# One decoder layer on Trainium2: split operands that stand still placed 64 bytes into their tiles, and the last two input blocks of the channel stage made earlier

## The chip, the cores and the metric

The kernel runs on one core of a Trainium2 chip. TensorE (PE) multiplies: an operand that stands still (stationary, at most 128 rows by 128 columns) is loaded into it, and another (moving, up to 512 columns) streams past. VectorE (DVE), ScalarE (ACT) and GpSimd (POOL) work on tiles in the on-chip memory, and DMA queues move data between it and the device's memory. The metric is the time of one execution on the device, in microseconds (us).

## The reference

```python
def reference(x, c, ...):                       # x (1, 2048, 1024) f32, D_FF = 2816
    mod = silu(c) @ w_ada + b_ada
    sh1, sc1, g1, sh2, sc2, g2 = split(mod, 6)
    u = rmsnorm(x, norm1_w) * (1 + sc1) + sh1
    hq, hf, hi, hg, aq, ak, av = split(u @ w_in)
    mix = concat([hgrn2(...), diff_attention(...)]) @ w_out
    h = x + g1 * mix
    u = rmsnorm(h, norm2_w) * (1 + sc2) + sh2
    ff = (silu(u @ w_ffn_gate) * (u @ w_ffn_up)) @ w_ffn_down
    return rmsnorm(h + g2 * ff, final_norm_w)
```

The mixer has a linear recurrence with four heads (hgrn2) and a differential attention with four heads. Everything is in 32-bit floats.

## The kernel before

**Split operands.** A 32-bit operand is cast to fp32r (the "high" part, ACT, L125), and DVE subtracts that from the operand for the "low" part (L126). A product is three matmuls: high by high, low by high, high by low. Both parts come from `split_tile`, whose tiles are 128 columns longer than their content. So where the content begins in its tile can be chosen, and the argument `moving` does that: content that moves begins SHIFT = 16 floats, which is 64 bytes, into the tile, and other content at the tile's start. As the program is laid out, every such tile itself begins at a multiple of 128 bytes. Only the weights that `load_half` makes for `proj_tf` (L195) are given moving=True: there 256 columns of weights move past, 64 bytes off, and 128 columns of an input stand still at a multiple of 128 bytes. In all other matmuls of split operands both begin at a multiple of 128 bytes. In the rows the moving operand is named first, then the one that stands still (ps_hg<-cuh,wh).

**The first half of the program** (up to 1401 us in the profile) computes projections, recurrence, attention and the output projection, on four blocks of 512 tokens, from block 3 to block 0. `proj_ft` (L183) is a projection with the weights standing still and 512 columns of the input moving, `proj_tf` (L195) one in pieces of 256 moving columns. `project_out(b)` writes block b of h to the device's memory, and `make_u2(b)` reads it back, norms it, transposes it on PE (128 x 128, L228), scales it (ACT L560, DVE L556) and writes u2 there as eight tiles (`u2_d`, L561).

**The second half** is the channel sub-layer, in two stages: s = 1 takes blocks 3 and 2, s = 0 blocks 1 and 0. Each stage has `combine(s)`, `activations(s)` and `down(s)`. The matrix products are done as two-by-two block products with seven multiplications instead of eight. `combine` makes the sums and differences of the u2 blocks that the seven products take: x, t2, t3, y, t1, w and t4, as split tiles named cx, ct2, ct3, cy, ct4, and cu for both t1 and w. `activations` goes over p = 0 to 10. For each p, `seven` runs on the gate's weights and then on those of the up projection. `seven` loads two strips of weights on SP's queue (r1, r2), builds sums s1 to s4 from them (buffers `wsum`), splits them (wa, ws, wt and the small wb), and runs seven products of 12 matmuls, 512 wide (L997), with the weights standing still and the combined inputs moving. The sums of products stand in PSUM banks: x and y in acc, t3 and t4 in sc, t1 and w in hg, t2 in tr or pv by turns. ws goes to t2 and t1, wt to t3 and w, wb to t4. `weights(p)`, in stage 1, also prepares the down projection's combined weights. `down(s)` takes the activations as the operand that stands still and the weights as the moving one (L1202), 77 steps of 24 matmuls, adds the residual, and does the final norm: squares with their sum on ACT (L1142), then scale and store.

**What sets the order.** Each engine takes its instructions in order. The program is written as generators that are interleaved by hand, and a list scheduler orders the instructions of each engine by estimated times before the program is built. In the second half the written order is: `combine(1)`, with most of it inside `project_out(0)`; `activations(1)`; `make_u2(1)`, `make_u2(0)`; `down(1)`, with `most` of `combine(0)` woven in; then `rest` of `combine(0)` beside the norms of stage 1; `activations(0)`; `down(0)`. As scheduled, the transposes of `make_u2(1)` and `make_u2(0)` stand among the first 160 matmuls of `down(1)`. SP's queue loads weights in order; POOL's queue stores.

Of the kernel before, what the change touches and what calls it, by code (L numbers as in the profile page):

```python
# [38 lines left out]
LAST = 2  # L39
LAST0 = 4  # L40
# [8 lines left out]
def kernel(ctx: ExitStack, tc: tile.TileContext, io: dict, out: bass.AP):  # L49
# [63 lines left out]
    u2_d = [[dram.tile([P, TB], F32, name=f"u2d{b}_{k}") for k in range(NK)] for b in range(NTB)]  # L113
# [110 lines left out]
    def transposed(k, xts, tags):  # L224
        pt = bank(*alternate("tr", *tags))
# [276 lines left out]
    def project_out(b, px, o, g1, take=None, tmp_=None):  # L502
# [11 lines left out]
        for k in range(NK):  # L514
            pt = transposed(k, ots, (("hg", 2),))
# [33 lines left out]
    def make_u2(b, px, take=None, tmp_=None):  # L549

        xts = normed(px, [h_d[b][tt * P:(tt + 1) * P] for tt in range(NT)], take)
        for k in range(NK):
            pt = transposed(k, xts, (("tr", 1), ("pv", 1)))
            ut = tmp_() if tmp_ else px.tile([P, TB], F32, name="t512", tag="t512", bufs=2)
# [6 lines left out]
            POOL.dma_start(out=u2_d[b][k], in_=ut)  # L561
# [309 lines left out]
    def combine(s):  # L871
# [15 lines left out]
        def load(kk, half, late, queue=SP):  # L887
            t = temp()
            queue.dma_start(out=t, in_=u2_d[2 * s + late][kk + 4 * half])
# [21 lines left out]
        def rest():  # L911
            for kk in range(4):
# [3 lines left out]
                put("w", kk, load(kk, 1, 1))  # L916
# [26 lines left out]
        return made, together(), most(), rest()  # L943
# [9 lines left out]
    def split_big(raw):  # L953
        wh, wl = (split_tile(pf, t, t, NW) for t in ("wh2", "wl2"))
# [12 lines left out]
    def seven(src, fs, u, finish):  # L967


# [4 lines left out]
        a11, a12 = r1[:, :TB], r1[:, TB:]  # L974
        a21, a22 = r2[:, :TB], r2[:, TB:]
        wa = split_big(r1)
        sa, sb = big("wsum", "wsum", 2), big("wsum", "wsum", 2)
        s1, s2, s3, s4 = sa[:, :TB], sa[:, TB:], sb[:, :TB], sb[:, TB:]
        DVE.tensor_tensor(s1, a21, a22, op=ALU.add)
        DVE.tensor_tensor(s2, s1, a11, op=ALU.subtract)  # L980
        ws = split_big(sa)
        DVE.tensor_tensor(s3, a11, a21, op=ALU.subtract)
        DVE.tensor_tensor(s4, a12, s2, op=ALU.subtract)
        wt = split_big(sb)
        wb = split_small(a22)
# [27 lines left out]
        finish(0, 0, px_, None)  # L1013
        product(pv_, half(ws, 0), "t1", True)
# [3 lines left out]
        t12 = temp()  # L1018
        DVE.tensor_tensor(t12, pv_, c12, op=ALU.add)
        finish(0, 1, None, t12)  # L1020
        product(pz, wb, "t4", False)
        DVE.tensor_tensor(c12, pz, c12, op=ALU.add)
        finish(1, 0, None, c12)
# [13 lines left out]
    def activations(s, u):  # L1037

        for p in range(NP):
# [11 lines left out]
            def other():  # L1051
                return ss.tile([P, TB], F32, name="asum", tag="asum", bufs=4)

            def up(j, t, ps, sb):
                a = sl[j, t]
                DVE.tensor_tensor(a, sb if ps is None else ps, a, op=ALU.mult)
                if (j, t) == (0, 0):
                    store(0, a)
                elif (j, t) == (1, 1):
                    store(5, a)  # L1060
                elif (j, t) == (0, 1):
                    s1, s2 = other(), other()
                    DVE.tensor_tensor(s1, a, sl[1, 1], op=ALU.add)
                    store(4, s1)
                    DVE.tensor_tensor(s2, s1, sl[0, 0], op=ALU.subtract)
                    store(1, s2)
# [218 lines left out]
```

## Time and profile before

| what | us |
| --- | --- |
| median of 3 runs | 2706.44 (2706.34 to 2708.68) |
| profiled execution | 2710.17 |
| its span in the profile | 2708.4 |
| PE busy in the span | 2605.8 (96%) |
| ACT, DVE busy in the span | 1144.6, 1826.3 |

The profiled execution took 1.8 us more than its span, and 3.7 us more than the median. The share of PE is so high that the time is PE's: its instructions one behind the other, and the few places where it stands. The second half of the span, by stage: `project_out(0)`, `make_u2(2)` and the start of `combine(1)` end at 1401 us; `activations(1)` runs to about 1829; `down(1)` to 2052; `activations(0)` to about 2484; `down(0)` to 2693.9; then 14.5 us without matmuls.

### The profile page before, as it was taken

To read this page: it belongs to the slowest core of one execution; us is meant where nothing else is said; L and a number is where in the kernel's file an instruction comes from. 1 tells how busy PE (TensorE), PEld (TensorE's weight loads), DVE (VectorE), ACT (ScalarE), POOL (GpSimd) and SP (SyncE) were. 2 spreads that over 40 slices of the span, in tenths; PEclk is the share of its full clock that TensorE was granted. 3 is DMA by queue.
4 is the path that set the end of the run, shared out by engine and by line. 5 is a ranking of instruction groups with operands and counts; after the bars stand their busy time and mean duration, and the time that the engine had idled before them with its cause. 6 is when DMAs were issued, how large, how long until landed. Compare 5 with 4: busy or idle time off the path is not lost.

```text
span 2708.4 us, 40567 instructions
## 1 busy us (share of the span) xinstructions
PE 2605.8 (96%) x14753; PEld 2267.6 (84%) x14753; DVE 1826.3 (67%) x3608; ACT 1144.6 (42%) x2050; POOL 385.6 (14%) x603
## 2 busy tenths in 40 slices
PE   6999989999999999898899999999998999999997
PEld 5888879999999998798888888887887888888886
DVE  7434457778778778865577777667778666665467
ACT  4542126665565565643343222235444222222434
POOL 2552200010100001012121111112002110001001
PEclk9999999999999999998999999999999999999999
DMA  8764672433334231456665444459656333235665
GB/s 281 262 218 167 220 241 83 148 99 111 108 110 154 77 98 47 137 184 221 200 217 167 167 167 156 139 192 342 221 185 220 113 106 98 101 109 205 199 187 179
DMA packets 333628, 449.17 MB, mean 166 GB/s; under 512 B 26810, under 2 KB 212460, under 8 KB 333300
## 3 DMA queue, kind: packets, MB, share of 16 engines
q1 hardware_dynamic: 295508, 324.39, 37.6%
q0 software_dynamic: 37920, 122.19, 11.9%
q8 instruction: 116, 1.90, 0.3%
q14 instruction: 84, 0.69, 0.1%
HBM read 326.41 MB, written 120.06 MB: 165 GB/s over the span
## 4 chain that ended last, share of the span: by engine, by line
PE 72%; DMA 4%; issue 4%; DVE 3%; ACT 1%; POOL 1%; SPq 1%; DVEq 0%; POOLq 0%; ACTq 0%
PE ps_hg L997 8%; PE ps_sc L997 8%; PE ps_acc L997 8%; PE ps_acc L195 8%; PE ps_acc L183 6%; PE ps_pv L654 4%; PE ps_sc L1202 4%; PE ps_acc L1202 4%; PE ps_hg L1202 3%; PE ps_tr L997 2%; PE ps_sc L624 2%; PE ps_tr L650 2%; PE ps_sc L625 2%; PE ps_pv L997 2%; PE ps_hg L716 2%
## 5 line engine op out<-in xcount | busy, mean ns | idle before, releaser
L125 ACT CAST wh<-wraw 128x1024 fp32r<-128x1024 f32 (+1 forms) x320 | 327.1, 1044 | 589.3 <-PE ps_hg L997 183.2
L126 DVE TENSOR_TENSOR wl<-wraw,wh 128x1024 fp32r<-128x1024 f32 (+1 forms) x320 | 383.7, 1213 | 187.9 <-ACT wh L125 186.0
L195 PE MATMUL ps_acc<-wh,uh 128*128 128x256 f32 x1040 | 294.6, 285 | 1.0 <-ACT uh L526 0.8
L195 PE MATMUL ps_acc<-wl,uh 128*128 128x256 f32 x1040 | 292.8, 283 | 2.6 <-DVE wl L126 2.6
L195 PE MATMUL ps_acc<-wh,ul 128*128 128x256 f32 x1040 | 291.5, 283 | 0.1
L125 ACT CAST wh<-wsum 128x1024 fp32r<-128x1024 f32 x88 | 92.6, 1053 | 310.5 <-PE ps_acc L997 129.7
L195 PEld LDWEIGHTS ps_acc<-wl,uh 128*128 128x128 f32 x1040 | 196.0, 189 | 5.3 <-DVE wl L126 2.8
L195 PEld LDWEIGHTS ps_acc<-wh,uh 128*128 128x128 f32 x1040 | 195.8, 189 | 4.0 <-ACT uh L526 1.6
L195 PEld LDWEIGHTS ps_acc<-wh,ul 128*128 128x128 f32 x1040 | 195.1, 189 | 2.6 <-DVE ul L527 0.3
L628 DVE CUSTOM_DVE_ANT_0 s<-ps_sc,dist,mx 128x512 f32<-128x512 f32 x192 | 143.5, 747 | 46.8 <-PE ps_sc L625 42.4
L633 ACT ACTIVATE s<-s,mx 128x2048 f32<-128x2048 f32 (+15 forms) x128 | 154.1, 1204 | 47.2 <-DVE mx L628 45.2
L654 PE MATMUL ps_pv<-vt,wt 128*128 128x128 f32 x1088 | 152.0, 280 | 2.8 <-ACT wt L652 2.2
L654 PEld LDWEIGHTS ps_pv<-vt,wt 128*128 128x128 f32 x1088 | 141.6, 195 | 10.3 <-ACT wt L652 4.9
L183 PE MATMUL ps_acc<-uh,wh 128*128 128x512 f32 x352 | 140.3, 400 | 1.3 <-ACT wh L125 1.3
L183 PE MATMUL ps_acc<-ul,wh 128*128 128x512 f32 x352 | 139.8, 398 | 0.6 <-DMA ul<-ud 0.6
L183 PE MATMUL ps_acc<-uh,wl 128*128 128x512 f32 x352 | 138.5, 395 | 1.1 <-DVE wl L126 1.1
L997 PE MATMUL ps_hg<-cuh,wh 128*128 128x512 f32 x352 | 137.2, 391 | 1.1 <-ACT cuh L125 0.8
L624 PE MATMUL ps_sc<-ks,q 128*128 128x512 f32 (+2 forms) x320 | 133.3, 419 | 4.4 <-DVE mx L628 3.6
L997 PE MATMUL ps_hg<-cul,wh 128*128 128x512 f32 x352 | 137.4, 390 | 0.1
L997 PE MATMUL ps_hg<-cuh,wl 128*128 128x512 f32 x352 | 137.1, 390 | 0.0
L652 ACT COPY wt<-ps_tr 128x512 f32<-128x512 f32 (+3 forms) x160 | 83.1, 520 | 108.1 <-PE ps_tr L650 106.8
L126 DVE TENSOR_TENSOR wl<-wsum,wh 128x1024 fp32r<-128x1024 f32 x88 | 107.3, 1221 | 29.9 <-ACT wh L125 29.1
(424 smaller groups left out, 6811.4 us busy)
## 6 DMA issues: line engine op xcount, KB each, us to landing
wraw<-in_w_in_dram SPq DMA_DIRECT2D x88, 512.0 KB, 4.0
wraw<-actd SPq DMA_DIRECT2D x154, 256.0 KB, 2.6
wraw<-in_w_ffn_gate_dram SPq DMA_DIRECT2D x44, 512.0 KB, 4.9
wraw<-in_w_ffn_up_dram SPq DMA_DIRECT2D x44, 512.0 KB, 3.6
actd<-t POOLq DMA_DIRECT2D x88, 256.0 KB, 3.1
wraw<-wdd SPq DMA_DIRECT2D x88, 256.0 KB, 4.0
actd<-asum POOLq DMA_DIRECT2D x66, 256.0 KB, 3.5
wraw<-in_w_ffn_down_dram SPq DMA_DIRECT2D x66, 256.0 KB, 4.0
```

Source lines behind the costliest of these rows:

```text
L125: ACT.copy(dst_h, src)
L126: DVE.tensor_tensor(dst_l, src, dst_h.bitcast(F32), op=ALU.subtract)
L183: PE.matmul(pa, a[:, k % 4, j * P:(j + 1) * P], c, start=n == 0, stop=n == 3 * NK - 1)
L195: PE.matmul(pa[:, j], a[:, tt * P:(tt + 1) * P], c[:, k % 4], start=n == 0, stop=n == 3 * NK - 1)
L624: PE.matmul(ps[:, :n], qs[m][0][:, qc], ks[m][pc][:, :n], start=True, stop=False)
L625: PE.matmul(ps[:, :n], qs[m][1][:, qc], ks[m][pc][:, :n], start=False, stop=True)
L628: DVE.tensor_tensor_reduce(out=s[:, lo:hi], in0=ps[:, :hi - lo], in1=dist[:, u0_:u0_ + hi - lo], op0=ALU.add, op1=ALU.min, scale=-slope, s ...
L633: ACT.activation(s[:, :W], s[:, :W], AF.Exp, scale=-1.0, bias=mx[:, npiece - 1:npiece], accum_out=mx[:, 4:5])
L652: ACT.copy(wt[:, :ge - g], pt[:, :ge - g])
L654: PE.matmul(pv[:, :P], wt[:, j - g], vq[j // 4][:, j % 4], start=j == 0, stop=j == i)
L997: PE.matmul(pa[:, cs], a, c[:, cs], start=first and i == 0, stop=i == 11 and cs.stop == TB, skip_group_check=not first)
L1202: PE.matmul(sets[n % 2][tt], a[x][:, tt * P:(tt + 1) * P], w[y], start=kk == 0 and m == 0 and n not in (2, 6), stop=kk == NP - 1 and m == ...
```

## The change

1. **Where split operands begin.** The argument is now `shift`, true unless told otherwise. Shifted by 64 bytes: all wide tiles of `load_half` (so also the weights that stand still in `proj_ft`, 960 matmuls), and the tiles of `split_big`, which are the weights that stand still in `seven` and the activations that stand still in `down`. The moving weights of `down` are not (`not w`), nor is the small wb of `seven` (product t4), nor are the moving inputs. `proj_tf` is as it was.
2. **u2 of blocks 1 and 0.** `make_u2(1)` and `make_u2(0)` before `down(1)` are gone. A new generator `u2_tile` makes one token tile (128 rows) of one block in each p = 2 to 9 of `activations(1)`: its norm ahead of the gate's `seven`, four transposes and four ACT scalings between gate and up, four more after up. `u2_d` has another layout, and is written in rows of 512 bytes.
3. **Weights ahead.** What `seven` did first (load, s1, s2, split of wa and ws) is `prepare`. For p = 0 it runs before the stage: in stage 1 before the last steps of `combine(1)`, in stage 0 inside `down(1)`.
4. **Rest of combine(0).** It falls into `last_w`, now inside `down(1)`, and `last_t1`, which runs with the norms of stage 1 in a callback after the first `seven` of `activations(0)` has split its weights.
5. **Order of the products in `seven`:** x, t2, t3, y, t1, w, t4 becomes x, t2, t3, y, t4, t1, w, with one more temporary (c21). In `up` the sums of the activations follow that order.
6. **Banks.** The transposes of `project_out(0)` alternate over hg, hg, sc, sc and not over hg alone.
7. LAST 2 to 1, LAST0 4 to 3, and another order of slots in `down`. Of PE's order at the end of both `down` stages these change nothing.

```diff
-LAST = 2
-LAST0 = 4
+LAST = 1
+LAST0 = 3
...
-    def split_tile(pool, name, tag, bufs, moving=False, wide=True):
-
-        n = moving * SHIFT
+    def split_tile(pool, name, tag, bufs, shift=True, wide=True):
+
+        n = (shift and wide) * SHIFT
         return pool.tile([P, D + wide * P], F32R, name=name, tag=tag, bufs=bufs)[:, n:n + D]
...
-            split_tile(pool, n, t, bufs, moving, wide).rearrange("p (k c) -> p k c", k=4)
+            split_tile(pool, n, t, bufs, True, wide).rearrange("p (k c) -> p k c", k=4)
...
-        def rest():
+        def last_w():
+            for kk in range(4):
+                put("w", kk, load(kk, 1, 1))
+                yield
+
+        def last_t1():
             for kk in range(4):
                 x, z = load(kk, 0, 0), load(kk, 0, 1)
                 DVE.tensor_tensor(x, z, x, op=ALU.subtract)
                 put("t1", kk, x)
-                put("w", kk, load(kk, 1, 1))
                 yield
...
-    def split_big(raw):
-        wh, wl = (split_tile(pf, t, t, NW) for t in ("wh2", "wl2"))
+    def split_big(raw, shift=True):
+        wh, wl = (split_tile(pf, t, t, NW, shift) for t in ("wh2", "wl2"))
...
+    def prepare(src, fs):
...
         wa = split_big(r1)
...
+        return r1, r2, wa, s2, split_big(sa)
...
+    def u2_tile(b, tt):
+        def take(dt=F32):
+            t = pf.tile([P, D], dt, name="xt1", tag="g1", bufs=1)
+            return t[:, :TB], t[:, TB:]
+
+        xt, = normed(ss, [h_d[b][tt * P:(tt + 1) * P]], take)
+        yield
+        for g, tag in enumerate(("tr", "pv")):
+            pt = bank(tag, 1, (4, P))
+            for k in range(4):
+                PE.transpose(out=pt[:, k], in_=xt[g][:, k * P:(k + 1) * P], identity=ident)
+            ut = other()
...
+            yield
...
             fs = (p, p + NP)
-            seven(w_gate, fs, u, gate)
+            q = p - 2
+            u2 = u2_tile(1 - q // 4, q % 4) if s and 0 <= q < 8 else iter(())
+            next(u2, None)
+            seven(first if p == 0 else prepare(w_gate, fs), u, gate, between if p == 0 else None)
             if s:
                 weights(p)
-            seven(w_up, fs, u, up)
+            next(u2, None)
+            seven(prepare(w_up, fs), u, up)
+            next(u2, None)
...
-                ops.append(split_big(raw))
+                ops.append(split_big(raw, not w))
...
+    weights0 = prepare(w_gate, (0, NP))
     run(steps)
-    activations(1, made)
-    make_u2(1, ss, slots(T3), temp)
-    make_u2(0, ss, slots(T2), temp)
-    made, _, most, rest = combine(0)
+    activations(1, made, weights0)
+    made, _, most, last_w, last_t1 = combine(0)
     steps = down_load(1, 0) + down_load(1, 2)
-    _, norms = down(1, steps, itertools.chain([None] * 8, most))
-    run(calls(*norms), rest)
-    activations(0, made)
+    weights0, norms = down(
+        1, steps, itertools.chain([None] * 8, most, [None] * 13, last_w), lambda: prepare(w_gate, (0, NP))
+    )
+    activations(0, made, weights0, lambda: run(calls(*norms), last_t1))
```

PE, end of `project_out(0)` (L195), where `make_u2(2)` (xt) and the transposes of the mixer's output (slot) stand between the matmuls. Before:

```order
L195 MATMUL ps_acc<-wh,slot 128x256 x2
L228 MATMUL ps_pv<-ident,xt 128x128 x4
L228 MATMUL ps_hg<-ident,slot 128x128 x4
L228 MATMUL ps_tr<-ident,xt 128x128 x4
L228 MATMUL ps_hg<-ident,slot 128x128 x4
L195 MATMUL ps_acc<-wh,slot 128x256
```

And in the changed kernel:

```order
L195 MATMUL ps_acc<-wh,slot 128x256 x2
L228 MATMUL ps_tr<-ident,xt 128x128 x4
L228 MATMUL ps_pv<-ident,xt 128x128 x4
L228 MATMUL ps_hg<-ident,slot 128x128 x8
L228 MATMUL ps_sc<-ident,slot 128x128 x8
L195 MATMUL ps_acc<-wh,slot 128x256
```

The 16 transposes of the mixer's output that stood in groups of four around matmuls stand together, on two kinds of bank, and 24 matmuls of L195 stand ahead of them where 12 did.

PE, start of `down(1)`; slot in L228 is the normed tile of `make_u2`, L997 the last products of `activations(1)`. Before:

```order
L1202 MATMUL ps_acc<-wl_19206,wh_19198 128x512
L1202 MATMUL ps_acc<-wh_19205,wl_19199 128x512
L228 MATMUL ps_tr<-ident,slot 128x128
L228 MATMUL ps_pv<-ident,slot 128x128
L1202 MATMUL ps_acc<-wl_19206,wh_19198 128x512
L997 MATMUL ps_hg<-cuh_15464,wh_18823 128x512
```

In the changed kernel the same place reads:

```order
L1235 MATMUL ps_acc<-wh_19221,wh_19214 128x512
L1235 MATMUL ps_acc<-wl_19222,wh_19214 128x512
L1235 MATMUL ps_acc<-wh_19221,wl_19215 128x512
L1006 MATMUL ps_hg<-cuh_15440,wh_19087 128x512
L1006 MATMUL ps_hg<-cul_15441,wh_19087 128x512
```

The 64 transposes of `make_u2(1)` and `make_u2(0)` are gone from here; as L1058, in eight pairs of groups of four, they stand between the products of `activations(1)`.

ACT, end of `down(1)` and start of `activations(0)`; the casts from wsum are those of the first ws and wt. Before:

```order
L125 CAST wh_21089<-wraw_21085 128x1024
L125 CAST wh_21097<-wsum 128x1024
L125 CAST sh<-wraw_21216 128x512
L1142 ACTIVATE junk,fss<-slot 128x512 x6
L125 CAST wh_21103<-wsum 128x1024
L125 CAST wh_21218<-wraw_21214 128x1024
L1142 ACTIVATE junk,fss<-slot 128x512
L125 CAST cuh_21036<-t_21034 128x512
```

In the changed kernel:

```order
L125 CAST wh_20993<-wraw_20989 128x1024
L125 CAST wh_21000<-wsum 128x1024
L125 CAST sh<-wraw_21232 128x512
L1175 ACTIVATE junk,fss<-slot 128x512 x4
L1015 COPY t_21144<-ps_acc 128x512
L1175 ACTIVATE junk,fss<-slot 128x512
L125 CAST wh_21031<-wsum 128x1024
L125 CAST wh_21234<-wraw_21230 128x1024
```

Ahead of the cast of wt there are now five of the norm's squares and the eviction of product x, where there were six squares. On PE the 12 matmuls of product y (cy) stand ahead of product t3, which takes wt; before they stood behind it.

## Rows read from the trace of the kernel before

**Rows 1.** The page: busy time of each engine and its share of the span.

```profile
PE 2605.8 (96%) x14753; PEld 2267.6 (84%) x14753; DVE 1826.3 (67%) x3608; ACT 1144.6 (42%) x2050; POOL 385.6 (14%) x603
```

**Rows 2.** Busy time by stretch: start:end, length, then the first line's columns.

```profile
core 0: us, PE busy (x) PEld busy (x) DVE busy (x) ACT busy (x) POOL busy (x), PEclk, DMA share, GB/s
1339.00:1362.00 23.00, 16.97 (x116) 15.64 (x115) 12.85 (x20) 10.05 (x18) 4.57 (x8) 0.85 0.47 161
1365.00:1400.00 35.00, 35.00 (x300) 35.00 (x299) 28.76 (x42) 11.10 (x15) 11.08 (x18) 1.00 0.69 236
1401.10:1432.00 30.90, 27.38 (x105) 19.57 (x104) 29.98 (x47) 18.07 (x29) 5.02 (x10) 0.94 0.60 188
1432.00:1823.00 391.00, 391.00 (x1744) 324.17 (x1743) 274.32 (x385) 110.77 (x148) 59.98 (x111) 1.00 0.49 164
1823.00:1892.00 69.00, 64.74 (x311) 52.18 (x309) 49.94 (x82) 42.60 (x72) 20.19 (x30) 1.00 0.95 351
2052.20:2095.00 42.80, 34.83 (x140) 26.84 (x140) 36.66 (x62) 19.32 (x35) 7.32 (x12) 0.92 0.58 190
2095.00:2480.00 385.00, 385.00 (x1718) 319.21 (x1717) 246.50 (x341) 107.08 (x141) 38.39 (x71) 1.00 0.31 105
```

**Rows 3.** Timeline of PE at the lower clock: start, us, engine, line, operation.

```profile
2065.99 0.63 PE L997 MATMUL ps_sc<-ct3l,wh 128*128 128x512 f32 x1
...
2067.26 0.63 PE L997 MATMUL ps_sc<-ct3l,wh 128*128 128x512 f32 x1
```

**Rows 4.** Timeline of PE at full clock, in down(0) and in activations(1).

```profile
2601.85 0.39 PE L1202 MATMUL ps_hg<-wh,wh 128*128 128x512 f32 x1
...
2603.89 0.39 PE L1202 MATMUL ps_acc<-wh,wh 128*128 128x512 f32 x1
...
1500.11 0.39 PE L997 MATMUL ps_sc<-ct4l,sh 128*128 128x512 f32 x1
...
1502.38 0.39 PE L997 MATMUL ps_sc<-ct4h,sl 128*128 128x512 f32 x1
```

**Rows 5.** Timeline of PE, L195: usual spacing, and the closest one.

```profile
1380.53 0.40 PE L195 MATMUL ps_acc<-wh,slot 128*128 128x256 f32 x2
...
1382.30 0.40 PE L195 MATMUL ps_acc<-wh,slot 128*128 128x256 f32 x2
...
452.43 0.28 PE L195 MATMUL ps_acc<-wh,uh 128*128 128x256 f32 x1
...
453.11 0.28 PE L195 MATMUL ps_acc<-wh,uh 128*128 128x256 f32 x1
```

**Rows 6.** Timeline of PE and DVE before the transposes of make_u2(2).

```profile
1352.77 0.44 PE L228 MATMUL ps_pv<-ident,xt 128*128 128x128 f32 x1 [4.05 <-DVE t L556]
...
1351.81 0.81 DVE L556 TENSOR_SCALAR t<-ps_pv,a,modc 128x512 f32<-128x512 f32 x1 [3.65 <-DMA u2d<-t]
```

**Rows 7.** What PE waited for, from 1395 us on: in total, times, longest.

```profile
PE ps_sc L997 <- ACT wh L125: 4.2, 1, 4.2
PE ps_acc L997 <- ACT t L1006: 2.8, 2, 1.8
PE ps_acc L1202 <- ACT wh L125: 1.5, 1, 1.5
PE ps_hg L1202 <- DVE wl L126: 1.5, 2, 1.2
...
PE ps_pv L1202 <- DVE t L556: 0.9, 1, 0.9
```

**Rows 8.** Timeline of ACT and of PE at the start of activations(0).

```profile
2056.58 0.63 ACT L1142 ACTIVATE junk<-slot 128x512 bf16<-128x512 f32 x1 [3.56 <-DVE slot L1135]
...
2060.98 1.03 ACT L125 CAST wh<-wsum 128x1024 fp32r<-128x1024 f32 x1
...
2057.49 0.39 PE L997 MATMUL ps_pv<-ct2h,wl 128*128 128x512 f32 x1
2062.06 0.79 PE L997 MATMUL ps_sc<-ct3h,wh 128*128 128x512 f32 x1 [4.18 <-ACT wh L125]
```

More of the change, by code (lines that the diff above doesn't have):

```diff
@@ L112 @@
     gate_d = [dram.tile([P, D], F32, name=f"gated{j}") for j in range(2)]
-    u2_d = [[dram.tile([P, TB], F32, name=f"u2d{b}_{k}") for k in range(NK)] for b in range(NTB)]
+    u2_d = [[dram.tile([P, 4, TB], F32, name=f"u2d{b}_{k}") for k in range(2)] for b in range(NTB)]
     act_d = [
@@ L224, in transposed @@
     def transposed(k, xts, tags):
-        pt = bank(*alternate("tr", *tags))
+        pt = bank(*alternate(tags, *tags))
         for tt in range(NT):
@@ L499, in run, with project_out @@
                 pass
-    def project_out(b, px, o, g1, take=None, tmp_=None):
+    def project_out(b, px, o, g1, take=None, tmp_=None, tags=(("hg", 2),)):
         def half():
@@ L547, in project_out, with make_u2 @@
             yield
-    def make_u2(b, px, take=None, tmp_=None):
-        xts = normed(px, [h_d[b][tt * P:(tt + 1) * P] for tt in range(NT)], take)
+    def make_u2(b, px, tags=(("tr", 1), ("pv", 1))):
+        xts = normed(px, [h_d[b][tt * P:(tt + 1) * P] for tt in range(NT)])
         for k in range(NK):
-            pt = transposed(k, xts, (("tr", 1), ("pv", 1)))
-            ut = tmp_() if tmp_ else px.tile([P, TB], F32, name="t512", tag="t512", bufs=2)
+            pt = transposed(k, xts, tags)
+            ut = px.tile([P, TB], F32, name="t512", tag="t512", bufs=2)
             if k % 2:
@@ L888, in load @@
             t = temp()
-            queue.dma_start(out=t, in_=u2_d[2 * s + late][kk + 4 * half])
+            queue.dma_start(out=t, in_=u2_d[2 * s + late][half][:, kk])
             return t
@@ L941, in together @@
                 yield
-        return made, together(), most(), rest()
+        return made, together(), most(), last_w(), last_t1()
     def big(name, tag, bufs, dt=F32):
@@ L1013, in seven @@
         finish(0, 0, px_, None)
+        product(pz, wb, "t4", False)
+        c21 = temp()
+        DVE.tensor_tensor(c21, pz, c12, op=ALU.add)
+        finish(1, 0, None, c21)
         product(pv_, half(ws, 0), "t1", True)
@@ L1017, in seven @@
         product(pv_, half(wt, 1), "w", False)
[L1018 to L1023, printed above, removed]
+        DVE.tensor_tensor(c12, pv_, c12, op=ALU.add)
+        finish(0, 1, None, c12)
     def weights(k):
@@ L1035, in weights, with other, activations @@
             POOL.dma_start(out=wd_d[n][k], in_=t)
-    def activations(s, u):
+    def u2_tile(b, tt):
[9 more added lines that the diff above has]
+            ut = other()
+            for k in range(4):
+                n = 4 * g + k
+                ACT.activation(
+                    ut[:, k * P:(k + 1) * P], pt[:, k], AF.Identity, bias=modc[:, SH2, n:n + 1], scale=a2[:, n:n + 1]
+                )
+            POOL.dma_start(
+                out=u2_d[b][g][:, :, tt * P:(tt + 1) * P], in_=ut.rearrange("p (k n) -> p k n", n=P)
+            )
+            yield
+    def other():
+        return ss.tile([P, TB], F32, name="asum", tag="asum", bufs=4)
+    def activations(s, u, first, between=None):
         for p in range(NP):
@@ L1116, in down @@
                 [bank("hg", 2), bank("hg", 2), bank("pv", 1), bank("tr", 1)]]
-        place = slots([f"u{z}{k}" for z in "hl" for k in range(NK)])
+        place = slots([f"u{z}{k}" for ks in (range(4, NK), range(4)) for z in "hl" for k in ks])
         ho = [[place() for tt in range(NT)] for t in range(2)]
@@ L1211, in down @@
             held = []
-            if n == 6 and k == 0 and not s:
+            if n == 6 and k == 0:
                 for tt in range(NT):
@@ L1216, in down @@
             pass
-        return made, [lambda t=t, tt=tt: norm(t, tt, POOL) for t in (1, 0) for tt in range(NT)] if s else []
+        return made, [lambda tt=tt: norm(0, tt, POOL) for tt in range(NT)] if s else []
     def calls(*fs):
```

64 lines of the change are left out of this document (29 added, 35 removed).

## The prediction, made before the changed kernel ran

> **What bounds the kernel now.** I began with busy time: PE is busy for 96% of the span, DVE for 67% and ACT for 42% [rows 1]. So two things can shorten the time: PE's matmuls coming closer together, and the few places where PE stands or runs at its lower clock. The table by stage shows where those places are [rows 2]. In 1432:1823 and in 2095:2480 PE is busy without a break at clock 1.00; there only the spacing of matmuls counts. It stands, or has a lower clock, in four short stretches: 1339:1362 (16.97 of 23.00 us busy, clock 0.85), 1401.1:1432 (27.38 of 30.90, 0.94), 1823:1892 (64.74 of 69.00) and 2052.2:2095 (34.83 of 42.80, 0.92). The change touches each of the four, and the spacing as well. From here on all is counted against the profiled execution: 2710.17 us, of which 1.8 lie outside its span. It stands 3.7 above the median; I carry the differences over to the median, 2706.44.
>
> **Part 1: where operands begin.** The first question is what a matmul takes beyond its columns. [...] But nine matmuls of L1202 take 2601.85 to 2603.89, which is 0.2267 each, and those of L997 lie as far apart, 10 in 2.27 [rows 4]. [...] I take -2.3, between the -2.0 and -3.3 that L195's usual spacing gives, since that is what hundreds of its rows show.
>
> How many matmuls change? By the program, 3124 of L997 at full width (44 sevens of 84, less t4's 528 and the 44 that are split in two), 1848 of L1202 (2 x 77 x 12), and 960 of L183, of which I count 800, since some stand behind other waits: 5770. At -2.3 ns that is **-13 us**; at the ends -38 and +54. Beyond the spacing the shift costs nothing: a split takes ACT and DVE the same on the tiles of L195, which are shifted already, and none is added.
>
> [...]
>
> **Part 2: the end of project_out(0), 1339:1362.** PE stood 4.05 us before transposes of `make_u2(2)`, released by DVE L556, which itself had waited 3.65 for a store of u2 to give back its buffer [rows 6]. In all PE stands for 6.0 us here, and the clock is down to 0.85 of 23.00 us, another 3.4 [rows 2]. After the change 24 matmuls of L195 stand ahead of these transposes where there were 12 (12 x 0.118 = 1.4 us of cover), and 16 transposes stand together on two kinds of banks, so none waits for the bank before. But u2 still has two buffers here, so the wait for the store may stay. Bounds 0 and -9 (all of 6.0 and 3.4); I take the middle, **-5**.
>
> **Part 3: start of activations(1), 1401.1:1432.** The first gate weights are prepared before the last steps of `combine(1)`. PE stands 3.5 us here, beside a DVE that is busy for 29.98 of 30.90 [rows 2]: it splits the combined inputs, and that stays. **0**, from -3 to +1.
>
> **Part 4: inside activations(1).** PE is busy 391.00 of 391.00 us [rows 2], so this can only lose. The 64 transposes cost the same here as where they were. ACT gets 64 small scalings, at 110.77 of 391 us busy; DVE gets the norms, at 274.32 of 391. Both have room. The risks are two. On SP's in-order queue the load of an h tile waits for its single buffer, and the weights of the next products are queued behind it. And the scheduler now lets the t2 product of one `seven` slip behind the x product of the next, so a weight buffer comes free only some 23 matmuls (5.2 us) before it is needed. Each p may lose about a us: 0 to +8. I take **+2**.
>
> **Part 5: start of down(1), 1823:1892.** PE stands 4.3 us: 1.5 for a cast of activations, 1.5 in two waits for the low parts, 0.9 for L556 [rows 2, 7]. DMA is at 0.95 here, with 351 GB/s, as 16 stores of u2 and the loads of the next inputs fall together. Transposes, ACT's and DVE's scalings, norms and stores move out of it; what moves costs PE the same in part 4, but the waits between go. Bounds -1 (only L556's) and -6; I take **-5**. The loads of `most` stay.
>
> **Part 6: start of activations(0), 2052.2:2095.** This is the largest. PE stood 4.18 us from 2057.49 until wt's cast, begun on ACT at 2060.98, since six squares of the final norm stood ahead of it from 2056.58 on [rows 7, 8]. Behind it the clock was at its lower level for a while: 0.92 over 42.80 us is 3.4 lost [rows 2]. Two waits for L1006's evictions add 2.8 [rows 7]. Now five squares and one eviction stand ahead of that cast, which is no shorter (about 0.75 us for each square with its read-out). But t3 is later in PE's row by the 12 matmuls of y: 12 x 0.2267 = 2.7 us. So of the 4.18, 1.5 stays. If the stop is that short the clock need not fall: -2.7 - 3.4 = **-6**. Bounds 0 (ACT is later by as much) and -10 (most of the 8.0 standing and half of the clock's loss).
>
> The last item of the list moves no instruction of PE at either end, so the last 14.5 us without matmuls stay.
>
> The schedule sums to -5 + 0 + 2 - 5 - 6 = **-14 us** (-28 to +8), the shift to -13: **-27**, 2706.4 - 27 = **2679 us**.
>
> **The rivals.**
> A. *Spacing doesn't change.* [...] 2706 - 14 = **2692**. [...]
> B. The forecast, 2679.
> [...]
> [...]
> E. *The change doesn't take the waits away.* The store that held L556 holds it still, ACT is late with wt all the same, and activations(1) stops where it didn't: schedule +8 and not -14. With B's spacing 2706 + 8 - 13 = 2701, with A's 2714.
>
> **How the numbers follow.** B 0.30, C 0.28, A 0.24, D 0.11, E 0.07. B and C are near to each other; B is the likeliest since it rests on L195's usual rows. The range is 2640 to 2702: from C with the better half of the schedule's bounds (-28) to A with the worse half (-14 + 10), leaving out D and E. A measurement of this kernel tells some 0.2%, 5.4 us, from no change: below 2701.0 is faster, above 2711.9 slower. B and C are faster but for 0.01. A's 0.24 is 0.20 faster, 0.03 same, 0.01 slower; D is 0.09 slower and 0.02 same; E is 0.03 faster, 0.02 same, 0.02 slower. Together 0.80 faster, 0.08 same, 0.12 slower.
>
> **What would show it.** *Shift*: the spacing of L1006 and L1235 (the lines' new numbers) in a stretch without waits. [...] The product t4 has neither operand shifted, so it must stay at 0.2267 beside its neighbours; if all move together it isn't the offset. *Part 5*: no transposes at the start of `down(1)`, DMA below 0.95. *Part 6*: no stop of 4 us after the t2 product, clock near 1.00 in the first 40 us. *Part 4*: PE busy below 100% in activations(1) would show the loss, with SP's or ACT's work named as the releaser. The forecast is wrong if the spacing falls by more than twice 2.3 ns or rises at all.

## The result, and the profile after

The changed kernel is slower: a median of 2742.60 us against 2707.51, a ratio of 1.0121 with a 95% interval of 1.0109 to 1.0134. The forecast was 2679, faster, in a range up to 2702; slower had got 0.12. The shift works the other way: it costs 32 us in a run below, between the forecast's -13 and the prediction's worse end of +54, and the schedule's gain of 14 did not come.

The page of the changed kernel (busy time, share of the span, instructions) shows PE busy for 34 us more than before, as much as the span grew by (2741.7 against 2708.4); no other engine gained more than 20 [rows 1]:

```profile
PE 2640.3 (96%) x14753; PEld 2268.5 (83%) x14753; DVE 1828.1 (67%) x3600; ACT 1164.4 (42%) x2106; POOL 387.9 (14%) x603
```

So PE did the same matmuls in more time; it doesn't stand more. The table by stretch, with the same stages as in [rows 2] (start:end, length, then the columns of the first line):

```profile
core 0: us, PE busy (x) PEld busy (x) DVE busy (x) ACT busy (x) POOL busy (x), PEclk, DMA share, GB/s
1339.00:1362.00 23.00, 18.73 (x155) 17.64 (x155) 12.38 (x20) 10.59 (x18) 4.68 (x8) 1.00 0.45 151
1400.40:1435.00 34.60, 24.91 (x77) 17.69 (x77) 27.75 (x48) 16.20 (x29) 7.65 (x13) 0.75 0.58 180
1435.00:1852.00 417.00, 417.00 (x1847) 337.63 (x1846) 294.08 (x424) 149.09 (x245) 76.17 (x134) 1.00 0.52 174
1852.00:1920.00 68.00, 66.00 (x284) 52.85 (x283) 48.09 (x59) 31.22 (x40) 3.25 (x6) 1.00 0.81 283
2073.10:2115.00 41.90, 36.27 (x148) 27.96 (x147) 35.95 (x60) 16.98 (x31) 9.00 (x13) 0.96 0.55 178
2115.00:2508.00 393.00, 393.00 (x1711) 317.81 (x1710) 246.81 (x335) 109.00 (x141) 37.90 (x70) 1.00 0.31 103
```

Two things are to be seen. Where PE is busy throughout at clock 1.00, it needs 393.00 us for 1711 recorded matmuls of `activations(0)`, where it needed 385.00 for 1718: the work that nothing hinders got slower. And of the four short stretches three got better (PE stands 4.3, 2.0 and 5.6 us in the first, third and fourth of them, where it stood 6.0, 4.3 and 8.0), but the start of `activations(1)` got worse: 9.7 us standing in place of 3.5, at clock 0.75.

The spacing itself, in the timeline of PE (start, us, engine, line, operation): a stretch of `down(0)`, one of `activations(0)`, and a product t4, the one whose operands are both unshifted.

```profile
2599.67 0.39 PE L1235 MATMUL ps_sc<-wh,wh 128*128 128x512 f32 x1
...
2603.87 0.39 PE L1235 MATMUL ps_sc<-wl,wh 128*128 128x512 f32 x1
...
2200.07 0.39 PE L1006 MATMUL ps_pv<-ct2h,wh 128*128 128x512 f32 x1
...
2205.66 0.39 PE L1006 MATMUL ps_sc<-ct3h,wh 128*128 128x512 f32 x1
...
2212.90 0.40 PE L1006 MATMUL ps_sc<-ct4h,sh 128*128 128x512 f32 x1
...
2214.29 0.39 PE L1006 MATMUL ps_sc<-ct4h,sh 128*128 128x512 f32 x1
...
2215.42 0.39 PE L1006 MATMUL ps_sc<-ct4h,sl 128*128 128x512 f32 x1
```

L1235: 18 matmuls in 4.20 us, 0.2333 each. L1006: 24 in 5.59, 0.2329. t4: its last 5 in 1.13, 0.226, as in [rows 4], but its first 6 in 1.39, 0.232. So the matmuls whose operand that stands still begins 64 bytes in take some 6 ns more, those of L1235 6.6. By the prediction's last line the forecast is wrong if the spacing rises at all. The control named there, t4, held in part. Of t4, in their midst and not shifted, only the last five matmuls are as fast as before: over all 44 products of t4 in the trace the mean spacing falls from 0.2328 after the first matmul to 0.2269 after the eighth, where before the change it was 0.2267 throughout.

What PE waited for from 1395 us on (total, times, longest), to be set beside [rows 7]:

```profile
PE ps_acc L1006 <- DVE wl L126: 4.2, 1, 4.2
PE ps_hg L1006 <- ACT cuh L125: 3.6, 2, 3.3
PE ps_hg L1006 <- DVE cul L126: 2.2, 1, 2.2
PE ps_acc L1006 <- ACT cxh L125: 2.2, 2, 1.7
PE ps_acc L1235 <- DVE wl L126: 2.0, 1, 2.0
PE ps_acc L1006 <- ACT t L1015: 2.0, 1, 2.0
```

The wait of 4.2 us for wt at the start of `activations(0)` is gone, as forecast. In its place stand waits at the start of `activations(1)`: 4.2 for the low part of the first up weights, 3.3 for cu and 1.7 for cx. Two questions follow: how much of the 35 us is the shift, and what the rest of the change, which did remove stops, is worth.

### The profile page after: what moved, and what is told of

It is laid out like the page before. It is cut to its first block, busy times and chain, and to the rows that moved or that the text cites. A ratio compares the mean times of both kernels' runs of the same rounds, so it can differ in the third digit from the quotient of the medians.

```text
span 2741.7 us, 40528 instructions
## 1 busy us (share of the span) xinstructions
PE 2640.3 (96%) x14753; PEld 2268.5 (83%) x14753; DVE 1828.1 (67%) x3600; ACT 1164.4 (42%) x2106; POOL 387.9 (14%) x603
## 4 chain that ended last, share of the span: by engine, by line
PE 73%; DMA 4%; issue 4%; DVE 4%; POOL 1%; ACT 1%; SPq 0%; DVEq 0%; POOLq 0%; ACTq 0%
PE ps_hg L1006 9%; PE ps_sc L1006 9%; PE ps_acc L1006 9%; PE ps_acc L195 8%; PE ps_acc L183 6%; PE ps_acc L1235 4%; PE ps_sc L1235 4%; PE ps_pv L654 4%; PE ps_hg L1235 3%; PE ps_tr L1006 2%; PE ps_pv L1006 2%; PE ps_sc L624 2%; PE ps_tr L650 2%; PE ps_sc L625 2%; PE ps_hg L716 2%
## 5 line engine op out<-in xcount | busy, mean ns | idle before, releaser
L125 ACT CAST wh<-wraw 128x1024 fp32r<-128x1024 f32 (+1 forms) x320 | 326.6, 1042 | 525.1 <-PE ps_hg L1006 112.7
L195 PE MATMUL ps_acc<-wh,uh 128*128 128x256 f32 x1040 | 294.0, 284 | 1.1 <-ACT uh L526 0.9
L195 PE MATMUL ps_acc<-wl,uh 128*128 128x256 f32 x1040 | 292.0, 282 | 2.5 <-DVE wl L126 2.5
L195 PE MATMUL ps_acc<-wh,ul 128*128 128x256 f32 x1040 | 290.8, 282 | 0.1
L195 PEld LDWEIGHTS ps_acc<-wl,uh 128*128 128x128 f32 x1040 | 195.3, 188 | 5.2 <-DVE wl L126 2.7
L195 PEld LDWEIGHTS ps_acc<-wh,uh 128*128 128x128 f32 x1040 | 194.9, 188 | 4.5 <-ACT uh L526 1.8
L195 PEld LDWEIGHTS ps_acc<-wh,ul 128*128 128x128 f32 x1040 | 194.4, 188 | 2.6 <-DVE ul L527 0.3
L654 PE MATMUL ps_pv<-vt,wt 128*128 128x128 f32 x1088 | 152.3, 280 | 2.5 <-ACT wt L652 1.7
L654 PEld LDWEIGHTS ps_pv<-vt,wt 128*128 128x128 f32 x1088 | 141.9, 195 | 10.3 <-ACT wt L652 4.4
L1006 PE MATMUL ps_hg<-cuh,wh 128*128 128x512 f32 x352 | 140.5, 400 | 3.6 <-ACT cuh L125 3.6
L183 PE MATMUL ps_acc<-ul,wh 128*128 128x512 f32 x352 | 140.9, 401 | 2.0 <-DMA ul<-ud 2.0
L1006 PE MATMUL ps_hg<-cul,wh 128*128 128x512 f32 x352 | 139.6, 397 | 2.2 <-DVE cul L126 2.2
L183 PE MATMUL ps_acc<-uh,wh 128*128 128x512 f32 x352 | 141.5, 404 | 0.0
L183 PE MATMUL ps_acc<-uh,wl 128*128 128x512 f32 x352 | 139.9, 399 | 0.8 <-DVE wl L126 0.8
L1006 PE MATMUL ps_hg<-cuh,wl 128*128 128x512 f32 x352 | 139.6, 397 | 0.0
L1085 POOL DMA_DIRECT2D actd<-t x88 | 47.8, 543 | 564.1 <-DVE t L1089 534.7
```

Source lines behind the costliest of these rows:

```text
L125: ACT.copy(dst_h, src)
L183: PE.matmul(pa, a[:, k % 4, j * P:(j + 1) * P], c, start=n == 0, stop=n == 3 * NK - 1)
L195: PE.matmul(pa[:, j], a[:, tt * P:(tt + 1) * P], c[:, k % 4], start=n == 0, stop=n == 3 * NK - 1)
L654: PE.matmul(pv[:, :P], wt[:, j - g], vq[j // 4][:, j % 4], start=j == 0, stop=j == i)
L1006: PE.matmul(pa[:, cs], a, c[:, cs], start=first and i == 0, stop=i == 11 and cs.stop == TB, skip_group_check=not first)
```

## The experiments

Theory 1 was: the shift costs 6.6 ns in every matmul whose two operands it set apart, and the rest of the change is about worth nothing. Theory 2, the rival: the moved work costs the time, and the looser spacing comes from it. Ratios are to the kernel before, on the same chip.

**The change without its shift, and the shift alone.** In e1_unshifted:

```diff
-    def split_tile(pool, name, tag, bufs, shift=True, wide=True):
+    def split_tile(pool, name, tag, bufs, shift=False, wide=True):
...
-            split_tile(pool, n, t, bufs, True, wide)
+            split_tile(pool, n, t, bufs, moving, wide)
```

(`split_big` likewise.) Expected:

> The changed kernel with every operand that stands still back at the start of its tile (only the weights of proj_tf stay 64 bytes in, as before). Theory 1 (the 64 bytes cost about 6.6 ns in each of some 5770 matmuls, 38 us, and the rest of the change is worth a few us): spacing of L1006 and L1235 0.2267, time 2703 to 2706, ratio to before 0.998 to 1.000. Theory 2 (the moved u2 work and the new order cost the time, and the looser spacing comes from them): spacing stays near 0.233 and the time near 2742.

In e2_shift_alone only the hunks of part 1 are put into the kernel before. Expected:

> The kernel before with part 1 alone: operands that stand still begin 64 bytes in, all else as it was. Theory 1: spacing of the seven's products and of down 0.2333, t4 0.2267, time 2707 + 36 to 40 = 2743 to 2747. Theory 2: within 5 us of 2707.

Measured: e1 2710.61 us, ratio 0.9999 (0.9986 to 1.0012); e2 2741.21, ratio 1.0119 (1.0102 to 1.0135). The timeline of PE in `down(0)`, e1 and then e2:

```profile
2601.41 0.39 PE L1235 MATMUL ps_acc<-wh,wl 128*128 128x512 f32 x1
...
2605.49 0.39 PE L1235 MATMUL ps_sc<-wh,wl 128*128 128x512 f32 x1
...
2599.83 0.39 PE L1202 MATMUL ps_acc<-wl,wh 128*128 128x512 f32 x1
...
2602.86 0.40 PE L1202 MATMUL ps_tr<-wh,wl 128*128 128x512 f32 x1
```

18 matmuls in 4.08 us, 0.2267, against 13 in 3.03, 0.233. The mean over the whole trace is 0.2267 for L1235 in e1; in e2 it is 0.2333 for L1202 and for the shifted products of L997. Theory 2 falls: the shift alone makes the whole loss, without the moved work, and the moved work without the shift makes none. Between the profiles, the time from the first product of `activations(0)` to the end of the span grew from 656.1 to 672.9 us in e2, 16.8, and 1562 + 924 shifted matmuls of 6.6 ns are 16.4 (924 is 77 steps of `down` with 12 matmuls each; the 24 to a step named at the start is too many). For the whole kernel the 2743 to 2747 expected were a little too much: 2710 x 0.0119 = 32 us and not 36 to 40. What is missing lies in the first half. L183, where all its weights are shifted (from 390 us on), takes 0.2332 in e2 against 0.2288 before, and yet the last attention matmul (L654) begins at 1284.4 us in e2 and at 1286.2 before. So the longer matmuls of L183 don't show in the time.

**Is it the place of one operand, or the distance between the two?** In e4_down_both the moving weights of `down` begin 64 bytes in as well:

```diff
-                ops.append(split_big(raw, not w))
+                ops.append(split_big(raw))
```

> The changed kernel, with the moving weights of down 64 bytes in as well, so that both operands of L1235 begin at the same place. If the distance between the two counts: L1235 falls from 0.2333 to 0.2267, 1848 matmuls, 12 us less than the changed kernel, 2730; L1006 stays at 0.2333. If the place of the operand that stands still counts by itself: L1235 stays at 0.2333 and the time at 2742.

Measured 2731.07 us, ratio 1.0080 (1.0064 to 1.0096), 11.5 below the changed kernel. The timeline of PE in `down(0)`:

```profile
2620.27 0.39 PE L1235 MATMUL ps_pv<-wh,wh 128*128 128x512 f32 x1
...
2622.99 0.39 PE L1235 MATMUL ps_hg<-wh,wl 128*128 128x512 f32 x1
```

12 matmuls in 2.72 us: 0.2267. With both operands 64 bytes in, the price is gone; L1006 stays at 0.2333 in the same run. It is the distance that costs, not the place of the operand that stands still.

**And where the kernel before has the shift, in L195?** e3_no_shift_at_all sets SHIFT = 0 in the kernel before.

```diff
-    SHIFT = 16
+    SHIFT = 0
```

> The kernel before with SHIFT = 0, so that the weights that move in proj_tf (L195, 256 columns) also begin at a multiple of 128 bytes, as the input that stands still does. If a distance of 64 bytes between moving and stationary operand is what costs: L195 falls from 0.1176 to 0.1133 a matmul, some 3800 of them, 10 to 17 us less, 2690 to 2697. If only the place of the operand that stands still counts, or if matmuls of 256 columns have another best place: 0.1176 or more, 2707 to 2717.

Measured 2716.86 us, ratio 1.0029 (1.0018 to 1.0039). The first branch, a gain, failed. The timeline of L195, to be set beside [rows 5]:

```profile
1382.01 0.40 PE L195 MATMUL ps_acc<-wh,slot 128*128 128x256 f32 x2
...
1384.53 0.40 PE L195 MATMUL ps_acc<-wh,slot 128*128 128x256 f32 x2
```

These are seven groups of three in 2.52 us: 0.1200, where 64 bytes apart give 0.1180. So for 256 columns 64 bytes save 2.0 ns, and for 512 they cost 6.6. This is what the forecast's step from one to the other could not see. The two differ in one more thing than the width: in L195 it is the moving operand that begins 64 bytes further in, in the shifted products the one that stands still. The next runs have distances at which that makes no difference, if distances count modulo 256 bytes.

**Which distances?** Three runs give the kernel before many offsets. e5_offsets mixes them within each product, e7_one_offset_each and e9_long_offsets have one for each group of matmuls.

In e5 (offsets in floats of 4 bytes, high and low part):

```diff
-        wa = split_big(r1)
+        wa = split_big(r1, (8, 4))
-        ws = split_big(sa)
+        ws = split_big(sa, (24, 12))
-        wt = split_big(sb)
+        wt = split_big(sb, (32, 20))
```

In e7:

```diff
-    def split_big(raw):
+    def split_big(raw, at=32):
...
-                ops.append(split_big(raw))
+                ops.append(split_big(raw, 0 if w else 8))
```

and in e9 the same with 64 and 112 in place of 32 and 8.

> The kernel before with many offsets at once, to read the spacing from one trace. Of the seven's weights that stand still: wa high 32 bytes, wa low 16, ws high 96, ws low 48, wt high 128, wt low 80; of down's: high 112, low 192; of the weights that move in L195: 32 or 128 bytes (high), 96 or 16 (low); everything else 0. If what counts is the distance between the running matmul's moving operand and the weights loaded behind it, modulo 128 bytes: next weights at 128 bytes behind a moving operand at 0 give 0.2267 as at 0, next weights at 192 give 0.2333 as at 64, and L195 at 128 gives 0.1195 as in the run without any shift. If it is the distance modulo a longer period: 128 and 192 bytes differ from 0 and 64. For 16, 32, 48, 80, 96 and 112 bytes no expectation but that they lie between 0.2133 and 0.240; if one gives below 0.2267, operands could be placed better than in either kernel.

> The kernel before, with one offset for each group of matmuls where e5_offsets mixed several: the seven's weights that stand still at 128 bytes (but t4's, at 0), down's at 32, proj_ft's (L183) at 96, and the weights that move in L195 at 128. In e5_offsets 128 bytes gave 0.2329 beside neighbours at other offsets. If what counts is the distance modulo 128 bytes, and e5's mixture disturbed it: L997 0.2267, L195 0.1195. If it is not a matter of 128 bytes (any offset that isn't 0 costs some 6 ns): L997 near 0.233. For 32 and 96 bytes, 0.231 to 0.236.

> As e7_one_offset_each, with longer offsets: the seven's weights that stand still at 256 bytes (t4's at 0), down's at 448, proj_ft's (L183) at 512, the weights that move in L195 at 256. In the kernels so far every pair at 0.2267 has its two operands a multiple of 512 bytes apart, since 128 columns of fp32r are 512 bytes, and every other distance up to 192 bytes cost 4 to 7 ns more. If the period is 512 bytes: L183 0.2275 as in the kernel before, L997 and L1202 0.231 to 0.234. If it is 256: L997 is 0.2267 too. If an offset just short of a period is better than 0: L1202 below 0.2267.

They took 2740.5, 2750.82 and 2720.46 us (one execution each). From the starts in their traces, and those of the runs above, the mean time from one matmul to the next of the same line, by how far into its tile the shifted operand begins. For 512 columns that is the operand that stands still, for 256 the one that moves. L183 is counted from 390 us on, where all its weights are shifted. Starts more than 15% above the usual spacing are left out, since those are waits. Means of e5 are marked as mixed; there neighbours stand at other offsets, and a mean moves by about 1 ns with the neighbour that one counts it to.

| bytes | 512 columns, ns | 256 columns (L195), ns |
| --- | --- | --- |
| 0 | 227.1 (L997), 226.9 (L1202) | 119.5 |
| 16 | 231.5 (mixed) | 118.3 (mixed) |
| 32 | 233.3 | 117.8 (mixed) |
| 48, 80 | 233.8, 231.0 (mixed) | |
| 64 | 233.3 | 117.6 |
| 96 | 233.7 (L183) | 117.7 (mixed) |
| 112 | 233.1 (mixed) | |
| 128 | 232.6 | 118.6 |
| 192 | 232.2 (mixed) | |
| 256 | 227.1 | 119.5 |
| 448 | 229.0 | |
| 512 | 228.6 (L183; at 0 bytes 228.8, at 64 233.2) | |

My guess of a period of 128 bytes failed in e5 already, and e7, without a mixture, gave the same: 232.6 ns at 128. The timeline of PE in `activations(1)` shows the 256 bytes of e9:

```profile
1500.08 0.39 PE L997 MATMUL ps_acc<-cyh,wh 128*128 128x512 f32 x1
...
1505.07 0.39 PE L997 MATMUL ps_hg<-cuh,wl 128*128 128x512 f32 x1
```

22 matmuls in 4.99 us: 0.2268. So the price is gone at 256 and at 512 bytes. That it depends on the distance modulo 256 alone is not shown: 448 is 192 more than 256, and its 229.0 isn't the 232.2 of the mixture at 192. In every other distance tried a matmul of 512 columns costs 2 to 7 ns more, and none is below 0's. In L195 every distance tried that isn't a multiple of 256 is 1 to 2 ns better. Which operand is ahead doesn't explain the change of sign, if distances count modulo 256 or 512. 128 bytes ahead and 128 behind are the same modulo 256, and there 512 columns lose 5.5 ns and 256 gain 0.9. And 448 bytes for 512 columns, which modulo 512 is where L195's operands stand with their 64, lose 2.1; that is the price to set beside L195's gain of 2.0, and 6.6 is the price in the other direction. So the kernel before had the better placing, of those tried, at either width.

**Where the gain of the moved work went.** By e1 the rest of the change is worth nothing, though three stretches improved. I compare how much each stretch loses in the profiled execution of each run: its length less its matmuls (counted in the program) at 0.2267, 0.1174 and 0.109 us for 512, 256 and 128 columns.

| us lost | before | e1 | e6 | e8 | e10 |
| --- | --- | --- | --- | --- | --- |
| last attention matmul (L654) to the start of activations(1) | 14.9 | 9.2 | 8.6 | 10.5 | 10.5 |
| first 40 us of activations(1) | 8.2 | 17.8 | 14.7 | 10.7 | 14.1 |
| these two together | 23.1 | 27.0 | 23.3 | 21.2 | 24.6 |
| rest of activations(1) | 0.5 | 1.6 | 1.6 | 1.6 | 0.5 |
| start of down(1), 68 to 69 us | 6.7 | 3.2 | 4.4 | 4.5 | 7.8 |
| start of activations(0), 43 to 44 us | 11.8 | 9.5 | 8.2 | 9.9 | 8.2 |

In e1 the start of `activations(1)` loses 9.6 us more, about what the other stretches gain. The first three rows have to be read together, since the stage begins 5.7 us earlier in e1, counted from the last attention matmul, and what PE waits for at its start needn't come earlier too. Together the two stretches lose 3.9 us more. The changed kernel's ACT shows one cause:

```profile
1407.74 0.62 ACT L125 CAST cxh<-t 128x512 fp32r<-128x512 f32 x1 [3.73 <-DMA t<-u2d]
1415.24 0.63 ACT L214 ACTIVATE junk<-xt 128x512 bf16<-128x512 f32 x1 [6.88 <-DMA xt<-hd]
...
1416.62 0.60 ACT L125 CAST cuh<-t 128x512 fp32r<-128x512 f32 x1
```

L214 are the squares of the norm of the first u2 tile. It is written for p = 2, but its buffer is free from the start, so the scheduler put its load and its norm at p = 0; ACT waited 6.88 us for that load, with the casts of cu and cx queued behind it, which PE needed. e6_first_tile_held takes away what made it early. It is e1 with the buffer held until p = 1 has its activations:

```diff
             seven(prepare(w_up, fs), u, up)
             next(u2, None)
+            if s and p == 1:
+                held = pf.tile([P, D], F32, name="xt1", tag="g1", bufs=1)
+                DVE.tensor_copy(out=held[:, :1], in_=sl[0, 0][:, :1])
```

> The changed kernel without the shift (as e1_unshifted), and with the first u2 tile's buffer held until the activations of p = 1 are there (one DVE copy of one column into it), so that its load and its norm can't be queued at the start of activations(1). Theory: in e1 the start of activations(1) lost some 9 us more than before since the squares of that norm wait 3 to 7 us on ACT for their DMA, with casts of the combined inputs queued behind them. Then the time falls by 6 to 9 us against e1, ratio to before 0.9965 to 0.998, and PE's stops <- ACT cuh at the start of activations(1) go. Rival (the start is late since DMA is full and the up weights come late, whichever block is loaded): gain below 3 us, ratio 0.999 to 1.000.

Measured 2707.66 us, ratio 0.9985 (0.9972 to 0.9998). PE's waits in the first 40 us of `activations(1)`, e6:

```profile
PE ps_acc L1006 <- DVE wl L126: 4.4, 1, 4.4
PE ps_pv L1006 <- ACT ct2h L125: 2.3, 1, 2.3
```

The waits for cu and most of that for cx are gone, and 3.1 us of the loss; but the gain is half of what I expected. The wait for the up weights' low part, 2.3 us in e1 and 4.2 in the changed kernel, is 4.4 here, and one for ct2 came up. The rival of that run was right on this other half. The second load of those weights, on SP's queue, before and in e6:

```profile
1398.88 0.37 SPq L950 DMA_DIRECT2D wraw<-in_w_ffn_up_dram  x1
1397.24 0.37 SPq L954 DMA_DIRECT2D wraw<-in_w_ffn_up_dram  x1
```

In e6 it is issued 2.6 us after the first product (1394.64), where before it was issued 2.3 us ahead of it (1401.14). But counted from the last attention matmul it is issued after 111.2 us in e6 and after 112.7 before: the load isn't later, the stage begins earlier (after 108.5 us and 114.9). So a good part of what the stretch before won is waited away here, and that the two together lose 23.3 in e6 and 23.1 before says that, with the norm out of the way, nothing was won or lost. The loads of u2 did get slower. The DMA parts of the answers for 1130 to 1395 us (KB each, median us to landing), before the change:

```profile
u2d<-t POOLq DMA_DIRECT2D x16, 256.0 KB, 2.8
t<-u2d POOLq DMA_DIRECT2D x6, 256.0 KB, 4.2
```

and in e6:

```profile
u2d<-t POOLq DMA_DIRECT2D x16, 256.0 KB, 3.5
t<-u2d POOLq DMA_DIRECT2D x6, 256.0 KB, 6.2
```

e8_first_tile_and_layout puts u2 back into pieces of 128 x 512 that lie together:

```diff
-    u2_d = [[dram.tile([P, 4, TB], F32, ...) for k in range(2)] for b in range(NTB)]
+    u2_d = [[dram.tile([4, P, TB], F32, ...) for k in range(2)] for b in range(NTB)]
```

> e6_first_tile_held, and u2 kept in the device's memory as before, each 128 x 512 tile in one piece (4 x 128 x 512 in place of 128 x 4 x 512). In e6 loads of u2 land after 6.2 us (median) in down(1) and 6.2 before 1395, where they took 3.9 and 4.2 before the change, and the first up weights come late beside them. Theory: the layout makes these transfers slower, and with it the start of activations(1); then they land after some 4 us again, PE's stop for the low part of the first up weights (4.4 us) shrinks below 2, and the time falls by 2 to 5 us against e6, ratio to before 0.997. Rival: the loads are slower because they fall together with others; then they stay at 6 us and the time within 1.5 us of e6.

Measured 2702.82 us, ratio 0.9971 (0.9959 to 0.9984). The same answers of e8, and PE's longest waits at the start of `activations(1)`:

```profile
u2d<-t POOLq DMA_DIRECT2D x16, 256.0 KB, 3.2
t<-u2d POOLq DMA_DIRECT2D x6, 256.0 KB, 4.7
```

```profile
PE ps_acc L1006 <- DVE wl L126: 2.3, 1, 2.3
PE ps_pv L1006 <- ACT ct2h L125: 1.3, 1, 1.3
```

The loads land earlier there, the wait halves to 2.3, which is not below the 2 expected, and the start loses 4.0 us less. Half of this is again a matter of when the stage begins: the second up load is issued 0.6 us after the first product, but 111.1 us after the last attention matmul, as in e6, and the two stretches together lose 2.1 less. The ratios of e6 and e8 lie 3.8 us apart, their intervals overlap, and their profiled executions took the same time (spans 2704.4 and 2704.6); so that the layout shortens the whole time is likely, and not shown. In `down(1)` the loads of u2 still took 5.8 us at the median (6.2 in e6, 3.9 before), so there the layout isn't what slows them; that part of the expectation failed. e8 has the lowest ratio of this study, 0.3% below the kernel before.

**u2 back in its old place.** e10_u2_old_place is e1 with `make_u2(1)` and `make_u2(0)` after `activations(1)` again:

```diff
+    make_u2(1, ss, take=slots(T3), tmp_=temp)
+    make_u2(0, ss, take=slots(T2), tmp_=temp)
     made, _, most, last_w, last_t1 = combine(0)
```

> The changed kernel without the shift (as e1_unshifted), and with the u2 of blocks 1 and 0 made where it was made before, after activations(1); the new layout of u2, the banks, the order of products, the weights made ahead stay. Theory: moving u2 brought two things that about cancel, a slower start of activations(1) (17.8 us lost against 8.2 before, part of it by the squares of the first tile's norm on ACT, part by the layout) and a faster start of down(1) (3 to 4 lost against 6.7). Then the start of activations(1) loses 11 to 14 us (the layout's part stays), down(1)'s start 6 to 7, and the time is within 3 us of e1: ratio to before 0.998 to 1.000. Rival: moving u2 is worth its price and what cancels it is another part of the change; then this kernel is slower than e1 by over 3 us.

Measured 2709.99 us, ratio 1.0004 (0.9993 to 1.0016), as the theory has it. The start of `activations(1)` loses 14.1, near e6's 14.7, and that of `down(1)` 7.8. So moving u2 gives 3 to 4.5 us at `down(1)`, costs 1.1 inside `activations(1)`, and, as it was done, 3.7 at its start, or 2.4 with the stretch ahead of it. The norm that waits on ACT eats the gain.

## Why the prediction was wrong, point by point

**The shift (forecast -13 us, measured +32).** The step that failed is "I take -2.3, between the -2.0 and -3.3 that L195's usual spacing gives, since that is what hundreds of its rows show". No run shows that term for 512 columns; the runs showed +6.6 in its place. It is an estimate of mine, and its two values follow from the trace before: at a granted clock of 0.50 512 columns take 0.4267 us (mean of 13 spacings of L997, no wait between), so half of that, 0.2133, and a quarter, 0.1067, are estimates of what 512 and 256 columns take by themselves at 1.00; 0.2267 [rows 4] lies 13.3 ns above the one and L195's 0.118 [rows 5] 11.3 above the other, and 11.3 less 13.3 is -2.0. The rows were read rightly but for one: of the 300 records in 35.00 us [rows 2] three began before the window, so the spacing is 0.1178 and not 0.1167, and -3.3 should have been -2.2. The difference within L195 is real: e3 gives -2.0 ns for the 64 bytes. But they are rows of 256 columns, and I carried their price over to 512 as one per matmul. At 512 it was +6.6 ns, within the prediction's ends (-38 and +54 us over 5770 matmuls, which is -6.6 to +9.4 ns each), and with the other sign. An estimate per 64 bytes that move past, 0.118/16 = 7.38 ns in L195, so 0.236 for 512 columns, gives the upper end and is nearer, though it isn't that either: 0.2333 is 7.29. The trace held no pair of 512 columns 64 bytes apart, and between such ends the row nearest in kind (512 columns, 0.2267 with the two operands a multiple of 512 bytes apart) argued for no sign. The lower end follows from the closest spacing of L195, 0.1133 in [rows 5], 6.7 above its estimate of 0.1067; it is of 256 columns too.

The count of matmuls held: 2486 in a stage at 6.6 ns are 16.4 us, and 16.8 were measured. That the spacing doesn't change (rival A) did not hold: with the distance as the only difference, L1235 took 0.2333 us in the changed kernel and 0.2267 in e4. What in PE takes that time, no run here shows.

**Part 2 (forecast -5).** About right for the stretch, and not for the time. From the last attention matmul to the start of `activations(1)` the loss fell from 14.9 to 9.2 us (e1). The wait for L556 shrank from 4.05 to 2.1 us in the changed kernel, and the clock stayed at 1.00 in 1339:1362. But the sum carried the -5 to the end, and the next stretch gave it back.

**Part 3 (forecast 0, bounds -3 and +1).** Wrong, and outside its bounds: +9.6 (e1). The step that failed is that parts 2 and 3 were added as if they were independent: the stage begins 5.7 us earlier in e1, counted from the last attention matmul, but the second load of the up weights is issued only 1.0 us earlier (111.7 against 112.7), and PE waits longer there. Of the 9.6, 5.7 stand against part 2's gain, and 3.9 are new. The text looked at DVE, and at what moves out of this stretch; it missed that a generator written for p = 2 is scheduled as soon as its buffer is free. The order of SP's queue had the load there, and ACT's the squares. In e6, where that norm is held, the 3.9 are gone (23.3 against 23.1 before), and with the old layout as well 1.9 are won (e8).

**Part 4 (forecast +2).** +1.1. Neither SP's queue nor the weight buffers made PE stand.

**Part 5 (forecast -5).** -3.5 (e1), -2.2 (e8). A wait for the low part of weights, 2.0 us in the changed kernel, stands in place of the waits in [rows 7].

**Part 6 (forecast -6).** -1.9 to -3.6 (e8, e6). The wait for wt is gone; product y waits 2.0 us for the eviction of x in its place, since the squares now stand ahead of that on ACT. The step that was mis-sized is the clock: the stretch still had 0.96, which is 1.7 us of its 41.9, and the forecast gave back all of the 3.4 us.

The schedule's sum was to be -14 and is 0, by one term: part 3 took what the others gave. Rival E (+8) was nearer to this than the forecast; of its three reasons one held in full, that `activations(1)` stops where it didn't.

## What to carry to other kernels

Place the two operands of a matmul by the width that will run, measured at that width: here, for 512 columns of fp32r, 0, 256 and 512 bytes apart are the best of the distances tried, and for 256 columns any other distance tried is better than 0 and 256 by 1 to 2 ns. When work is written into a later loop step, look at when its first buffer is free, and what stands behind its first wait on each in-order engine, since a scheduler may put it at the start. When two neighbouring stretches are priced, ask whether what the second waits for comes earlier too; if not, the gain of the first is waited away there. And where the ends of an estimate have both signs, as -38 and +54 us here, no typical row of another shape decides between them.

## What the runs showed of the hardware that was not expected

The distance between the moving and the stationary operand changes the time of a matmul at full clock (granted 1.00). For 512 columns it is 0.2267 us at 0 and 256 bytes, at 512 the same as at 0 (L183), and 0.229 to 0.234 at ten distances that are not multiples of 256. The sign turns with the width: for 256 columns it is 0.1195 at 0 and 256, and 0.1176 to 0.1186 else. Shifting both operands alike brings it back (e4: 0.2267). At the lower clock it cost nothing. Six matmuls of the changed kernel with their weights 64 bytes in, at a granted clock of 0.50:

```profile
1413.66 0.63 PE L1006 MATMUL ps_acc<-cxh,wh 128*128 128x512 f32 x1
...
1415.79 0.63 PE L1006 MATMUL ps_acc<-cxh,wl 128*128 128x512 f32 x1
```

These are 5 spacings in 2.13 us, 0.426 each; the unshifted weights in [rows 3], at 0.50 as well, give 3 in 1.27, 0.423. Over all matmuls of the seven products at 0.50 that no wait holds, the mean is 0.4267 in either kernel. Why the distance matters, these runs don't settle: they show where the operands stood and what it cost.

After a run of shifted products the unshifted t4 doesn't start at 0.2267: the first six of its twelve take 1.39 us (2212.90 to 2214.29), 0.232 each, the next five 0.226, and the mean over all 44 of them goes the same way. So the time of these matmuls depends on those ahead of them as well.
